# A layer norm with GELU: its last 128 rows as two half tiles, the first of them kept off one DMA engine

## The chip, the cores and the metric

The kernel runs on one core of one Trainium2 chip. The metric is the time of one execution in device microseconds (us), as the median of several executions. A profile of one execution shows a span from the first to the last instruction that is about 1.8 us shorter than the time. All timed runs compared here were at the full granted clock (1.0). Ratios are the mean time of one kernel's fast runs over that of the kernel before in the same rounds, so they are not quite the ratio of the medians that are quoted.

## The reference, cut to what matters

```python
x: (8, 1024, 2048) float32          # 8192 rows of 2048, 8 KB each
normalized = (x - mean(x)) / sqrt(var(x) + eps)     # per row
out = gamma * normalized + beta
return 0.5 * out * (1 + tanh(sqrt(2 / pi) * (out + 0.044715 * out ** 3)))
```

67.1 MB are read and 67.1 MB written.

## The kernel before

The rows are worked on in tiles of 128 rows by 128 partitions. Four tiles (512 rows) are a block; each partition of a block holds four neighbouring rows, 32 KB. Five block buffers (`xts`, "slots") rotate. SyncE loads a block once the store that used its slot has landed; ScalarE issues the stores. VectorE takes the statistics of a tile and scales by gamma, GpSimd raises the variance to the power -1/2, ScalarE normalizes, TensorE adds beta and the scaled tile in PSUM, ScalarE applies the GELU and writes back into the slot.

```python
R = 4                                    # tiles in a block
SLOTS = 5
...
xg = xf.rearrange("(b p r) d -> b p r d", p=P, r=R)
...
@block.sync
def _(sy):
    for b in range(B):                   # B = 16 blocks
        s = slot(b)
        if stored(b):
            sy.wait_ge(s_store[s], stored(b))
        ...
        if b:
            sy.dma_start(out=xts[s], in_=xg[b]).then_inc(s_load[s], 16)
...
@block.scalar                            # the last block's stores go out tile by tile
    if by_row(b):
        ins.then_inc(s_r, 1)
        ac.dma_start(out=og[b, :, q:q + 1], in_=xt[:, q:q + 1])._wait_ge(
            s_r, b + q + 1).then_inc(s_store[slot(b)], 16)
    elif q == R - 1:
        ins.then_inc(s_r, 1)
        ac.dma_start(out=og[b], in_=xt)._wait_ge(s_r, b + 1).then_inc(s_store[slot(b)], 16)
```

## Time and profile before

| | before |
|---|---|
| time, median (before the prediction, 3 runs) | 319.74 us |
| DMA engines | at the top digit in 38 of 40 slices |
| busiest compute engine | VectorE, 83% |
| last store issued | 305.3 us |
| last completion of that store | 316.5 us |

The lines that carry the argument stand in the prediction. One part of the page adds to them. It lists the kinds of transfers: what goes where, issuer, count, size of one, and the median time from issue to landing.

```profile
xt<-in_x_dram SPq DMA_DIRECT2D x15, 4096.0 KB, 24.3
out_dram<-xt ACTq DMA_DIRECT2D x15, 4096.0 KB, 37.0
xt<-in_x_dram SPq DMA_DIRECT2D x4, 1024.0 KB, 8.1
out_dram<-xt ACTq DMA_DIRECT2D x4, 1024.0 KB, 12.7
```

A store of 1 MB needs about 2.5 us of all sixteen engines (eight packets of 309 ns on each), yet lands 12.7 us after its issue: it stands in a queue. I judged that handing over work sooner would not shorten such a tail, and that evening out what the sixteen engines still have to do could.

### The profile page before, as it was taken

The numbers are of one execution on the slowest core, as the hardware profiler recorded it, in microseconds if no ns is written. First come the engines' busy times: TensorE is split into PE (matmuls) and PEld (weight loads), VectorE is DVE, ScalarE is ACT, GpSimd is POOL, SyncE is SP. The second block draws the span as 40 slices with busy tenths as digits, with TensorE's granted clock in tenths as the row PEclk, the third lists the DMA queues.
The fourth block names the chain that finished last, engine by engine and source line by source line (L and its number), as shares of the span: only waits on it lengthen the run. The fifth ranks groups of instructions, "written<-read, shape, count | busy, mean of one in ns | idle before, by whom it ended". The sixth has DMA issues, their size and how long they took to land.

```text
span 317.8 us, 2075 instructions
## 1 busy us (share of the span) xinstructions
PE 244.3 (77%) x520; PEld 57.1 (18%) x520; DVE 265.0 (83%) x514; ACT 253.9 (80%) x132; POOL 79.0 (25%) x73
## 2 busy tenths in 40 slices
PE   2769988888888898888877868598595895868810
PEld 1211222111212122211111111122121111112100
DVE  3499999999999999999969799696996969879500
ACT  2679999999999999999969779696995969968920
POOL 1033323232323231323213222231312213212000
DMA  7999999999999999999999999999999999999994
GB/s 291 438 462 396 459 396 445 412 454 404 458 400 459 422 437 445 412 450 408 458 417 441 437 421 454 404 458 412 450 433 425 450 408 450 408 458 421 437 404 206
DMA packets 5571, 134.27 MB, mean 423 GB/s; under 512 B 656, under 2 KB 704, under 8 KB 704
## 3 DMA queue, kind: packets, MB, share of 16 engines
q1 hardware_dynamic: 2736, 67.11, 49.4%
q10 hardware_dynamic: 2832, 67.13, 49.1%
q14 instruction: 3, 0.02, 0.0%
HBM read 67.13 MB, written 67.11 MB: 422 GB/s over the span
## 4 chain that ended last, share of the span: by engine, by line
DMA 44%; DVE 27%; ACT 19%; PE 3%; issue 2%; ACTq 1%; DVEq 0%; SPq 0%
DMA out_dram<-xt 27%; DVE sts L148 15%; DMA xt<-in_x_dram 15%; ACT yk L201 12%; DVE zg L164 9%; ACT xt L208 7%; PE ps L226 2%; DMA rows<-in_gamma_dram 2%; DVE mvs L157 2%; DVE nms L141 1%; ACTq L216 1%; DVE ves L158 1%; PE ps L243 1%; ACT g_t L197 1%; ACTq L211 0%
## 5 line engine op out<-in xcount | busy, mean ns | idle before, releaser
L148 DVE BATCH_NORM_STATS2 sts<-xt 128x6 f32<-128x512 f32 x256 | 163.5, 681 | 23.7 <-DMA xt<-in_x_dram 21.7
L201 ACT ACTIVATE yk<-xt,nms,rss 128x2048 bf16<-128x2048 f32 x64 | 134.1, 2095 | 41.7 <-DVE nms L141 41.2
L243 PE MATMUL ps<-zg,ident 128*128 128x512 bf16 x256 | 120.8, 627 | 50.9 <-DVE zg L164 50.9
L132 POOL TENSOR_TENSOR rss<-ves,mhalf 128x1 f32<-128x1 f32 x64 | 78.0, 1219 | 216.5 <-DVE ves L158 157.0
L239 PE MATMUL ps<-b_hl,ones_b 33*128 33x512 bf16 x256 | 120.6, 624 | 2.2 <-PEq L234 2.2
L208 ACT ACTIVATE xt<-ps 128x2048 f32<-128x2048 f32 x64 | 118.8, 1857 | 1.5 <-PE ps L243 1.5
L164 DVE TENSOR_TENSOR zg<-yk,g_t 128x2048 bf16<-128x2048 bf16 x64 | 78.0, 1218 | 5.0 <-ACT yk L201 3.0
L243 PEld LDWEIGHTS ps<-zg,ident 128*128 128x128 bf16 x256 | 27.6, 130 | 144.1 <-DVE zg L164 108.7
L239 PEld LDWEIGHTS ps<-b_hl,ones_b 33*128 33x128 bf16 x256 | 27.0, 127 | 92.1 <-issue 88.4
L157 DVE BATCH_NORM_AGGREGATE mvs<-sts 128x2 f32<-128x24 f32 x64 | 16.9, 264 | 2.2
L141 DVE TENSOR_SCALAR nms<-mvs,rss 128x1 f32<-128x1 f32 x64 | 12.6, 196 | 0.0
L226 PE MATMUL ps<-rows,ones 1*128 1x512 f32 x8 | 7.2, 1072 | 6.0 <-DMA rows<-in_gamma_dram 6.0
L158 DVE TENSOR_SCALAR ves<-mvs 128x1 f32<-128x1 f32 x64 | 9.8, 154 | 2.2
L194 ACT ACTIVATE b_hl<-rows 1x2048 bf16<-1x2048 f32 x1 | 1.9, 1909 | 4.9 <-DMA rows<-in_beta_dram 4.9
L226 PEld LDWEIGHTS ps<-rows,ones 1*128 1x128 f32 x8 | 2.5, 323 | 9.2 <-DMA rows<-in_gamma_dram 6.0
L172 DVE TENSOR_TENSOR b_hl<-rows,b_hl 1x2048 bf16<-1x2048 f32 x1 | 2.3, 2281 | 2.1 <-ACT b_hl L195 2.1
L197 ACT ACTIVATE g_t<-ps 128x2048 bf16<-128x2048 f32 x1 | 1.9, 1877 | 2.4 <-PE ps L226 2.4
L190 ACT ACT_TABLE_LOAD x1 | 1.3, 1283 | 0.9 <-SPq L106 0.9
L167 DVE MEMSET b_hl<- 33x1024 uint32 x1 | 0.9, 912 | 1.2 <-SPq L106 1.2
L195 ACT ACTIVATE b_hl<-rows 1x2048 bf16<-1x2048 f32 x1 | 1.9, 1908 | 0.0
L123 POOL MEMSET ones<- 65x128 f32 x1 | 0.2, 202 | 0.5 <-SPq L106 0.5
L127 POOL TENSOR_SCALAR_AFFINE_SELECT ident<-ident 128x128 bf16<-128x128 bf16 x1 | 0.3, 294 | 0.1
(7 smaller groups left out, 0.9 us busy)
## 6 DMA issues: line engine op xcount, KB each, us to landing
xt<-in_x_dram SPq DMA_DIRECT2D x15, 4096.0 KB, 24.3
out_dram<-xt ACTq DMA_DIRECT2D x15, 4096.0 KB, 37.0
xt<-in_x_dram SPq DMA_DIRECT2D x4, 1024.0 KB, 8.1
out_dram<-xt ACTq DMA_DIRECT2D x4, 1024.0 KB, 12.7
rows<-in_beta_dram ACTq DMA_DIRECT2D x2, 8.0 KB, 5.6
rows<-in_gamma_dram ACTq DMA_DIRECT2D x1, 8.0 KB, 5.0
```

The source lines that it names most:

```text
L132: po.tensor_tensor(out=rss[:, c], in0=ves[:, c], in1=mhalf, op=ALU.pow)._wait_ge(s_a, k + 1).then_inc(s_q, 1)
L141: ve.tensor_scalar(out=nms[:, c], in0=mvs[:, q, 0:1], scalar1=rss[:, c], scalar2=-1.0, op0=ALU.mult, op1=ALU.mult)._wait_ge(s_q, count).th ...
L148: ins = ve.bn_stats(out=sts[:, q, j, :], in_=xr[:, j, :])
L157: ve.bn_aggr(out=mvs[:, q], in_=sts[:, q])._wait_ge(s_o, count + 1).then_inc(s_o, 1)
L158: ve.tensor_scalar(out=ves[:, q:q + 1], in0=mvs[:, q, 1:2], scalar1=float(eps), scalar2=1.0, op0=ALU.add, op1=ALU.mult)._wait_ge(s_o, coun ...
L164: ve.tensor_tensor(out=zgs[q % 2], in0=yks[q % 2], in1=g_t, op=ALU.mult)._wait_ge(s_n, count).then_inc(s_z, 1)
L197: ac.activation(out=g_t, in_=pss[0], func=ACT.Identity)._wait_ge(s_tg, 1).then_inc(s_c, 1)
L201: ac.activation(out=yks[t % 2], in_=xts[slot(b)][:, q], func=ACT.Identity, scale=rss[:, q:q + 1], bias=nms[:, q:q + 1])._wait_ge(s_p, t + ...
L208: ins = ac.activation(out=xt[:, q], in_=pss[i % 2], func=ACT.Gelu_apprx_tanh)._wait_ge(s_t, i + 1)
L226: ins = pe.matmul(pss[0][:, cols(j)], lhsT=ones[64:65], rhs=rows[64:65, j * K // nsub:(j + 1) * K // nsub, :d // K], start=True, stop=True)
L239: ins = pe.matmul(ps[:, cols(j)], lhsT=ones_b, rhs=b_hl[:, cols(j)], start=True, stop=False)
L243: ins = pe.matmul(ps[:, cols(j)], lhsT=ident, rhs=zgs[k % 2][:, cols(j)], start=False, stop=True)
```

## The change

The intent is to even out the engines at the end. The last 128 rows are worked on as two half tiles of 64 rows. Of the first half 60 rows go through one transfer and 4 rows through another: fifteen engines with four rows each and four engines with one row each. So one engine loads and stores four rows fewer than it did. The second half is spread over all sixteen engines (16 updates with data). It needs a 65th step of every compute engine, and a load that waits for one more slot.

```diff
+H = 64
+E = 4
...
+    def halves(v, a, h):
+        return [(v[n1:n1 + H - E], a[32:32 + H - E]), (v[n1 + H - E:n1 + H], a[0:4 * E:4]),
+                (v[n1 + H:n1 + 2 * H], h[32:32 + H])]
...
-                    if b:
+                    if 0 < b < B - 1:
                         sy.dma_start(out=xts[s], in_=xg[b]).then_inc(s_load[s], 16)
+                        if s == slot(B - 1):
+                            sy.sem_inc(s_tail, 32)
+                sy.dma_start(out=x_end[:, :R - 1], in_=last(xf)).then_inc(s_load[slot(B - 1)], 16)
+                for v, a in x_half[:2]:
+                    sy.dma_start(out=a, in_=v).then_inc(s_tail, 16)
+                sy.wait_ge(s_store[slot(B)], stored(B))
+                sy.dma_start(out=x_half[2][1], in_=x_half[2][0]).then_inc(s_load_h, 16)
...                                  # one more step on GpSimd, VectorE, ScalarE and TensorE
+                        for k, (v, a, se) in enumerate(outs[i]):
+                            dma = ac.dma_start(out=v, in_=a)
+                            if k == 0:
+                                dma._wait_ge(s_r, n_r)
+                            dma.then_inc(se, 16)
```

More of the change, by code (lines that the diff above doesn't have):

```diff
@@ L38, with last @@
     og = of.rearrange("(b p r) d -> b p r d", p=P, r=R)
+    n0 = n - P * R
+    n1 = n0 + P * (R - 1)
+    def last(v):
+        return v[n0:n1].rearrange("(p r) d -> p r d", p=P)
+    def halves(v, a, h):
+        return [(v[n1:n1 + H - E], a[32:32 + H - E]), (v[n1 + H - E:n1 + H], a[0:4 * E:4]),
+                (v[n1 + H:n1 + 2 * H], h[32:32 + H])]
     bf16 = mybir.dt.bfloat16
@@ L70 @@
     s_first = [sem(f"first{q}") for q in range(R)]
+    s_tail = sem("tail")
+    s_load_h = sem("load_h")
+    s_half = sem("half")
     s_load = [sem(f"load{s}") for s in range(SLOTS)]
@@ L98, in cols, with parts @@
         return slice(j * FMAX, (j + 1) * FMAX)
-    def by_row(b):
-        return b == B - 1
+    def parts(b):
+        return R + 1 if b == B - 1 else 1
     def stored(b):
-        return sum(16 * (R if by_row(c) else 1) for c in range(b) if slot(c) == slot(b))
+        return sum(16 * parts(c) for c in range(b) if slot(c) == slot(b))
+    tiles = [xts[slot(b)][:, q] for b in range(B) for q in range(R)] + [xts[slot(B)][:, 0]]
+    n_t = len(tiles)
+    x_end = xts[slot(B - 1)]
+    x_half, o_half = halves(xf, x_end[:, R - 1], tiles[-1]), halves(of, x_end[:, R - 1], tiles[-1])
+    outs = {R * b + R - 1: [(og[b], xts[slot(b)], s_store[slot(b)])] for b in range(B - 1)}
+    for q in range(R - 1):
+        outs[n_t - 1 - R + q] = [(last(of)[:, q:q + 1], x_end[:, q:q + 1], s_store[slot(B - 1)])]
+    outs[n_t - 2] = [(v, a, s_store[slot(B - 1)]) for v, a in o_half[:2]]
+    outs[n_t - 1] = [(v, a, s_half) for v, a in o_half[2:]]
     with tc.tile_critical(no_gpsimd_drain=True):
@@ L128, in _, with power @@
                                  pattern=[[-1, P]], channel_multiplier=1)._wait_ge(s_setp, 1).then_inc(s_setp, 1)
+                def power(t, count):
+                    c = slice(t % R, t % R + 1)
+                    po.tensor_tensor(out=rss[:, c], in0=ves[:, c], in1=mhalf,
+                                     op=ALU.pow)._wait_ge(s_a, count).then_inc(s_q, 1)
                 with po.Fori(0, B):
                     for k in range(R):
-                        c = slice(k, k + 1)
-                        po.tensor_tensor(out=rss[:, c], in0=ves[:, c], in1=mhalf,
-                                         op=ALU.pow)._wait_ge(s_a, k + 1).then_inc(s_q, 1)
+                        power(k, k + 1)
                     po.sem_inc(s_a, -R)
+                power(n_t - 1, 1)
             @block.vector
@@ L142, in mean, with step @@
                                      op0=ALU.mult, op1=ALU.mult)._wait_ge(s_q, count).then_inc(s_p, 1)
-                def step(s, q, wait, count, before, count_q, count_n):
-                    xr = xts[s][:, q].rearrange("p (s f) -> p s f", f=FMAX)
+                def step(x, q, wait, count, before, count_q, count_n):
+                    xr = x.rearrange("p (s f) -> p s f", f=FMAX)
                     for j in range(nsub):
@@ L151, in step @@
                                 ins._wait_ge(*wait)
-                                if wait[0] is s_load[s]:
-                                    ins.then_inc(s_load[s], -16)
+                                if wait[0] not in s_first:
+                                    ins.then_inc(wait[0], -wait[1])
                             if before is not None:
@@ L168, in _ @@
                 for q in range(R):
-                    step(slot(0), q, (s_first[q], 16), 2 * q, q - 1 if q else None, q, q)
+                    step(tiles[q], q, (s_first[q], 16), 2 * q, q - 1 if q else None, q, q)
                     if q == 0:
@@ L180, in _ @@
                         s, q = divmod(k, R)
-                        step(s, q, (s_load[s], 16) if q == 0 else None, 2 * k, (q - 1) % R, k + 1, k + 1)
+                        wait = (s_load[s], 16) if q == 0 else (s_tail, 32) if (s, q) == (slot(B - 1), R - 1) else None
+                        step(xts[s][:, q], q, wait, 2 * k, (q - 1) % R, k + 1, k + 1)
                     ve.sem_inc(s_o, -2 * SLOTS * R)
@@ L184, in _ @@
                     ve.sem_inc(s_n, -SLOTS * R)
-                mean(R - 1, 1)
-                scale(R - 1, 1)
+                step(tiles[-1], 0, (s_load_h, 16), 0, R - 1, 1, 1)
+                mean(0, 2)
+                scale(0, 2)
             @block.scalar
@@ L197, in _ @@
                 ac.activation(out=g_t, in_=pss[0], func=ACT.Identity)._wait_ge(s_tg, 1).then_inc(s_c, 1)
-                for t in range(T + 1):
-                    if t < T:
-                        b, q = divmod(t, R)
-                        ac.activation(out=yks[t % 2], in_=xts[slot(b)][:, q], func=ACT.Identity, scale=rss[:, q:q + 1],
-                                      bias=nms[:, q:q + 1])._wait_ge(s_p, t + 1).then_inc(s_n, 1)
+                n_r = 0
+                for t in range(n_t + 1):
+                    if t < n_t:
+                        c = slice(t % R, t % R + 1)
+                        ac.activation(out=yks[t % 2], in_=tiles[t], func=ACT.Identity, scale=rss[:, c],
+                                      bias=nms[:, c])._wait_ge(s_p, t + 1).then_inc(s_n, 1)
                     i = t - 1
@@ L205, in _ @@
                         continue
-                    b, q = divmod(i, R)
-                    xt = xts[slot(b)]
-                    ins = ac.activation(out=xt[:, q], in_=pss[i % 2], func=ACT.Gelu_apprx_tanh)._wait_ge(s_t, i + 1)
-                    if by_row(b):
+                    ins = ac.activation(out=tiles[i], in_=pss[i % 2], func=ACT.Gelu_apprx_tanh)._wait_ge(s_t, i + 1)
+                    if i in outs:
                         ins.then_inc(s_r, 1)
-                        ac.dma_start(out=og[b, :, q:q + 1], in_=xt[:, q:q + 1])._wait_ge(
-                            s_r, b + q + 1).then_inc(s_store[slot(b)], 16)
-                        ac.sem_inc(s_g, 1)
-                    elif q == R - 1:
-                        ins.then_inc(s_r, 1)
-                        ac.dma_start(out=og[b], in_=xt)._wait_ge(s_r, b + 1).then_inc(s_store[slot(b)], 16)
+                        n_r += 1
+                        for k, (v, a, se) in enumerate(outs[i]):
[3 more added lines that the diff above has]
+                            dma.then_inc(se, 16)
                         ac.sem_inc(s_g, 1)
@@ L234, in _, with summed @@
                 pe.sem_inc(s_g, 2)
+                def summed(t, count):
+                    ps, zg = pss[t % 2], zgs[t % 2]
+                    for j in range(nsub):
+                        ins = pe.matmul(ps[:, cols(j)], lhsT=ones_b, rhs=b_hl[:, cols(j)], start=True, stop=False)
+                        if j == 0:
+                            ins._wait_ge(s_g, count)
+                    for j in range(nsub):
+                        ins = pe.matmul(ps[:, cols(j)], lhsT=ident, rhs=zg[:, cols(j)], start=False, stop=True)
+                        if j == 0:
+                            ins._wait_ge(s_z, count)
+                    ins.then_inc(s_t, 1)
                 with pe.Fori(0, B):
                     for k in range(R):
-                        ps = pss[k % 2]
-                        for j in range(nsub):
-                            ins = pe.matmul(ps[:, cols(j)], lhsT=ones_b, rhs=b_hl[:, cols(j)], start=True, stop=False)
-                            if j == 0:
-                                ins._wait_ge(s_g, k + 1)
-                        for j in range(nsub):
-                            ins = pe.matmul(ps[:, cols(j)], lhsT=ident, rhs=zgs[k % 2][:, cols(j)],
-                                            start=False, stop=True)
-                            if j == 0:
-                                ins._wait_ge(s_z, k + 1)
-                        ins.then_inc(s_t, 1)
+                        summed(k, k + 1)
                     pe.sem_inc(s_g, -R)
                     pe.sem_inc(s_z, -R)
+                summed(n_t - 1, 1)
+        nc.gpsimd.wait_ge(s_half, 16)
         for b in range(B, B + SLOTS):
```

## The prediction

> **What bounds the kernel now.** I read the page first, for which engine is full, and then the last 60 us in finer stretches, because the change touches only the last block of rows.
>
> ```profile
> PE 244.3 (77%) x520; PEld 57.1 (18%) x520; DVE 265.0 (83%) x514; ACT 253.9 (80%) x132; POOL 79.0 (25%) x73
> ...
> DMA  7999999999999999999999999999999999999994
> ...
> HBM read 67.13 MB, written 67.11 MB: 422 GB/s over the span
> ```
>
> The first row gives the busy time of each engine. None reaches 84%. The DMA row is at its top digit in every slice but the first and the last. So the transfers are the bound from end to end: 134.2 MB through 16 DMA engines. The packet records of the trace give the pace: a packet of 8 KB (one row) takes 309 ns, and one of 32 KB (four rows of one partition) takes 1213 ns. Each engine moves 512 rows in and 512 out; 1024 times 0.303 us is 310 us, which is nearly the span of 317.8. VectorE, ScalarE and TensorE matter only if they hand over a store too late. The end shows they don't:
>
> ```profile
> 300.20 1.23 DVE L164 TENSOR_TENSOR zg<-yk,g_t 128x2048 bf16<-128x2048 bf16 x1 [3.00 <-ACT yk L201]
> ...
> 303.41 1.88 ACT L208 ACTIVATE xt<-ps 128x2048 f32<-128x2048 f32 x1 [1.48 <-PE ps L243]
> 305.32 0.34 ACTq L211 DMA_DIRECT2D out_dram<-xt  x1
> ```
>
> (Timeline: start, length, what.) The last arithmetic ends at 305.3 and the last store is issued there, yet the span runs for 12.5 us more. That time is the queue of stores draining. How it drains is the view that matters here (stretches; the last two columns are the mean busy share of the 16 DMA engines and GB/s):
>
> ```profile
> core 0: us, PE busy (x) PEld busy (x) DVE busy (x) ACT busy (x) POOL busy (x), PEclk, DMA share, GB/s
> ...
> 312.00:313.00 1.00, 0.00 (x0) 0.00 (x0) 0.00 (x0) 0.00 (x0) 0.00 (x0) 1.00 1.04 442
> 313.00:314.00 1.00, 0.00 (x0) 0.00 (x0) 0.00 (x0) 0.00 (x0) 0.00 (x0) 1.00 0.43 180
> 314.00:315.00 1.00, 0.00 (x0) 0.00 (x0) 0.00 (x0) 0.00 (x0) 0.00 (x0) 1.00 0.12 49
> 315.00:316.00 1.00, 0.00 (x0) 0.00 (x0) 0.00 (x0) 0.00 (x0) 0.00 (x0) 1.00 0.12 49
> 316.00:317.00 1.00, 0.00 (x0) 0.00 (x0) 0.00 (x0) 0.00 (x0) 0.00 (x0) 1.00 0.00 0
> ```
>
> The reader is to see 0.12 from 314 to 316: 0.12 times 16 is 1.9, so **two** engines still work while fourteen are done. The 16 completions of the last store say the same: fourteen fall between 313.71 and 314.22 us, the last two at 316.39 and 316.50. The final packets of the two late engines end at 316.06, within 10 ns of each other; those of the others end between 313.3 and 313.9. The delay is about 2.2 us, seven to eight packets of 8 KB. From the last completion to the end of the span it is a fixed 1.3 us. So the most that any rebalancing of the last rows can bring is about 2.2 us of 319.7, **0.7%**.
>
> [...] The kernel before has only 16-way transfers (each completion count has 16 steps that come with the data), so its trace cannot confirm the other cases.
> [...]
>
> **The change part by part.**
> - *Rows taken from engine 15.* It loads and stores 4 rows fewer: 8 packets of 309 ns, **-2.47 us** on that engine. That is just the delay seen (2.2 us), so I take this to be the intent.
> - *Rows given to engines 0 to 3.* One row in and one out each: +0.62 us. Their end moves from at most 313.9 to about 314.5.
> - *More transfers.* The last block was one load and four stores; it is now four loads and six stores (three rows per partition in one load, then 60, 4 and 64 rows; stores of three full tiles, 60, 4 and 64). Successive transfers show gaps of some 75 ns on an engine in the packet records at some ends. As an estimate, three extra on a typical engine cost 0.2 us, and five on engines 0 to 3 cost 0.4 us. Smaller packets: eight of 32 KB take 9.70 us; eight of 24 KB (0.91 us each, interpolated from 309 and 1213 ns) plus eight of 8 KB take 9.76 us. That is +0.06 us.
> - *One more tile of arithmetic.* A half tile costs an engine as much as a full one[...]: four statistics of 0.69 us, 0.26, 0.15, 0.20 and 1.23 on VectorE, about 4.2 us; 2.1 and 1.86 on ScalarE. Stores of the last tiles were issued at 293.26, 297.61, 301.97 us, so 4.35 us apart. In the worst case the last store slips from 305.3 to 309.7.
> - *Loads come in another order.* The last block's load was issued at 255.76 and landed at 279.96; VectorE idled 2.57 us for it. Behind the previous load (259.1) the three-row part needs eight turns of 0.91 + 1.21 us, so it lands at about 276 to 277.6. VectorE is free at 277.5, so tile 60 starts some 2.5 us earlier. The 60 rows then take four turns of 0.31 + 1.21 us, landing near 282, the last 64 rows near 288 to 290; tiles 63 and 64 are due at about 290 and 295. The last load also waits for a store that landed at 275.1; that is in time. So the last store should be issued near 307 and 309.7 at the latest.
> - *Is the drain starved?* Before the last 64 rows, the engines have work until about 312.4 (313.6 less four packets). A store issued at 307 to 309.7 is in time. The extra tile lies beside the draining stores and costs nothing.
>
> Sum by engine, last packet: typical engines 313.6 + 0.3 = 313.9; engines 0 to 3 about 314.6 to 314.9; engine 15, if late, 316.06 - 2.47 + 0.3 = 313.9; the **other late engine 316.06 + 0.3 = 316.3, if nothing else changes for it**.
>
> **The rivals.**
> (a) *The second straggler sets the end.* It has the same end as the first and keeps its work, so the time stays within 0.3 us of before: about 319.9. For it: the completions of the last seven stores each show two late engines, about 2 us behind. Against it: the author moved rows off one engine only[...]. The second one's delay may also belong to this execution: in the stores of blocks landing up to 117 us only one engine is late, and the second appears after.
> (b) *Only engine 15 matters, or the two delays hang together*, so that relief for one relieves the other. For it: the two reach the same end within 10 ns. Then engines 0 to 3 set the end, near 314.6 to 314.9, that is 1.2 to 1.5 us earlier: about 318.4.
> (c) *Arithmetic becomes the bound.* If the late loads slip by over 3 us, the last store comes too late and the end moves out by as much: 320 to 322. Against it is the slack of 2.7 us or more worked out above.
> (d) *The odd transfers are slow.* 60 partitions on fifteen engines is a shape that nothing in this trace shows. If it ran on far fewer engines, a single engine would have to move many rows at 0.31 us each, and the time would rise by 2 us or more.[...]
>
> **Range and chances.** I give (a) 0.45, (b) 0.42, and (c) and (d) together 0.13. That puts the middle at **319.2 us**, with 318.0 to 320.3 as the range for 8 times in 10. A gain over 2% would need 6.4 us, three times the whole tail, and a loss over 2% a serious failure of (c) or (d). So faster 0.01, same 0.98, slower 0.01.
>
> **What would show it.** In the last stretches: one engine left (a share near 0.06 for about 1.5 us) means (a); a share that falls to 0.25 or less for only half a microsecond (engines 0 to 3) and an end near 315 means (b). In the timeline, tile 60's statistics should start near 277.5 and the last store be issued between 307 and 309.7; a DMA share below 0.9 between 295 and 312 means (c). Landing times of the 60-row load and store far over those of the 64-row ones mean (d). The prediction is wrong if the late engines turn out not to be slow by themselves but late through something that the new order moves, or if the last arithmetic starves the drain.

The sum came to 319.2 us, with the last packets at 313.9 us on a typical engine, 314.6 to 314.9 on engines 0 to 3, 313.9 on engine 15 and 316.3 on the other late one. That the four engines are 0 to 3, and that the spared one is engine 15, was my assumption. The traces show only how many engines a transfer uses. Engine numbers in this document are labels from the first experiment: engine k - 1 is the one that a small load of k rows is the first to reach. The "turns" of a load's and a store's packet are my estimate, from the two queues' shares of the engines' time before (49.4% and 49.1%, page of the kernel before).

## The result, and the profile after

The time is 319.81 us (319.68 to 320.18, 6 runs) against 319.71 us before (6 runs). The ratio is 1.0002, with a 95% interval of 0.9989 to 1.0015. The change moves the time by nothing that can be seen.

First the timeline of the end of the changed kernel (start, length, engine, line, what):

```profile
302.70 1.23 DVE L206 TENSOR_TENSOR zg<-yk,g_t 128x2048 bf16<-128x2048 bf16 x1 [2.99 <-ACT yk L246]
...
306.06 1.88 ACT L251 ACTIVATE xt<-ps 128x2048 f32<-128x2048 f32 x1 [1.63 <-PE ps L286]
307.97 0.59 ACTq L256 DMA_DIRECT2D out_dram<-xt  x1
```

The 65th step costs nothing: the last store goes out 2.65 us later than before, and the engines still have work. Then the drain, in the same stretches and columns as in the prediction (the last two are the DMA share and GB/s):

```profile
312.00:313.00 1.00, 0.00 (x0) 0.00 (x0) 0.00 (x0) 0.00 (x0) 0.00 (x0) 1.00 0.95 401
313.00:314.00 1.00, 0.00 (x0) 0.00 (x0) 0.00 (x0) 0.00 (x0) 0.00 (x0) 1.00 0.61 254
314.00:315.00 1.00, 0.00 (x0) 0.00 (x0) 0.00 (x0) 0.00 (x0) 0.00 (x0) 1.00 0.22 90
315.00:316.00 1.00, 0.00 (x0) 0.00 (x0) 0.00 (x0) 0.00 (x0) 0.00 (x0) 1.00 0.12 49
316.00:317.00 1.00, 0.00 (x0) 0.00 (x0) 0.00 (x0) 0.00 (x0) 0.00 (x0) 1.00 0.00 0
```

The share of 0.12 from 315 to 316 is still there: two engines work while the others are done, just as before. What changed is the stretch from 314 to 315, where 0.22 (3.5 engines) stands in place of 0.12: the engines that took over the four rows. The sixteen completions of the last store tell the rest. A completion is one of the sixteen updates of the transfer's semaphore; in the kernel before, the last two came 0.3 and 0.4 us after the last packets ended (316.06). They come from the trace, sorted; they carry no engine numbers. (In the kernel before, the tile stores share one semaphore, so two of the values near 314 are late completions of the store ahead; which two cannot be seen.)

```
before   313.71 ... 314.22 (fourteen)                                      316.39  316.50
changed  311.68   313.82 ... 314.10 (ten)   314.48  315.04  315.09         316.45  316.66
```

One engine is now done 2.1 us ahead of all others. By the change that is the engine which the 60 rows spare, engine 15 in the prediction: it alone has less to do. Eight packets of 309 ns are 2.47 us, and 311.68 + 2.47 is 314.15, just after the pack of ten. So the spared engine was not among the late two before, and the two that were late still are. My first reading was then: **the change relieves an engine that was not late.** Three things had to be tested: which engines are late, whether the relief does anything, and what makes an engine late.

### The profile page after: what moved, and what is told of

Read it like the earlier page. It is cut to its first block, busy times and chain, and to the rows that moved or that the text cites. A ratio compares the mean times of both kernels' runs of the same rounds, so it can differ in the third digit from the quotient of the medians.

```text
span 317.9 us, 2115 instructions
## 1 busy us (share of the span) xinstructions
PE 248.0 (78%) x528; PEld 58.1 (18%) x528; DVE 269.2 (85%) x522; ACT 257.7 (81%) x134; POOL 79.5 (25%) x74
## 3 DMA queue, kind: packets, MB, share of 16 engines
q1 hardware_dynamic: 2899, 67.11, 49.4%
## 4 chain that ended last, share of the span: by engine, by line
DMA 43%; DVE 27%; ACT 21%; PE 2%; issue 2%; ACTq 2%; DVEq 0%; SPq 0%
DMA out_dram<-xt 26%; DVE sts L190 15%; DMA xt<-in_x_dram 15%; ACT yk L246 13%; ACT xt L251 8%; DVE zg L206 8%; PE ps L269 2%; DMA rows<-in_gamma_dram 2%; DVE mvs L199 2%; ACTq L256 2%; DVE nms L183 1%; DVE ves L200 1%; ACT g_t L241 1%; ACTq L260 0%; DVEq L220 0%
## 5 line engine op out<-in xcount | busy, mean ns | idle before, releaser
L190 DVE BATCH_NORM_STATS2 sts<-xt 128x6 f32<-128x512 f32 x260 | 165.9, 679 | 22.1 <-DMA xt<-in_x_dram 19.8
L246 ACT ACTIVATE yk<-xt,nms,rss 128x2048 bf16<-128x2048 f32 x65 | 136.1, 2093 | 40.4 <-DVE nms L183 39.9
L286 PE MATMUL ps<-zg,ident 128*128 128x512 bf16 x260 | 122.7, 627 | 49.6 <-DVE zg L206 49.6
L282 PE MATMUL ps<-b_hl,ones_b 33*128 33x512 bf16 x260 | 122.5, 624 | 2.2 <-PEq L277 2.2
L251 ACT ACTIVATE xt<-ps 128x2048 f32<-128x2048 f32 x65 | 120.6, 1856 | 1.6 <-PE ps L286 1.6
L206 DVE TENSOR_TENSOR zg<-yk,g_t 128x2048 bf16<-128x2048 bf16 x65 | 79.2, 1219 | 5.0 <-ACT yk L246 3.0
```

Source lines behind the costliest of these rows:

```text
L190: ins = ve.bn_stats(out=sts[:, q, j, :], in_=xr[:, j, :])
L206: ve.tensor_tensor(out=zgs[q % 2], in0=yks[q % 2], in1=g_t, op=ALU.mult)._wait_ge(s_n, count).then_inc(s_z, 1)
L246: ac.activation(out=yks[t % 2], in_=tiles[t], func=ACT.Identity, scale=rss[:, c], bias=nms[:, c])._wait_ge(s_p, t + 1).then_inc(s_n, 1)
L251: ins = ac.activation(out=tiles[i], in_=pss[i % 2], func=ACT.Gelu_apprx_tanh)._wait_ge(s_t, i + 1)
L282: ins = pe.matmul(ps[:, cols(j)], lhsT=ones_b, rhs=b_hl[:, cols(j)], start=True, stop=False)
L286: ins = pe.matmul(ps[:, cols(j)], lhsT=ident, rhs=zg[:, cols(j)], start=False, stop=True)
```

## The experiments

**1. Which engines are late.** Sixteen small loads were put at the end of ScalarE's queue, behind the stores. The k-th has k rows and a semaphore of its own.

```diff
+    probe = sb("probe", [16, 16 * 128], f32)
...
+                for k in range(1, 17):
+                    ac.dma_start(out=probe[0:k, (k - 1) * 128:k * 128], in_=xf[0:k, 0:128]).then_inc(s_probe[k], 16)
```

> The kernel before, with sixteen small loads at the very end of the ScalarE queue; the k-th one reads k rows of 512 bytes into k partitions and counts on a semaphore of its own[...], behind all stores of that queue. The first k whose completions hold a late one (near 316 us, when the others are near 314) names the first late engine; the k at which a second late one joins names the second. Theory 1 (the late engines are those that also carried instruction fetches): two late engines, and engine 15 is not among them, so the late count is the same for k = 15 and k = 16. [...] The time rises by 1 to 3 us from the extra issues.

(What could be tested of the second theory, that engine 15 is late, is that the late count would rise at k = 16.)

The run was correct and took 322.8 us. The completions that came with data were, in us:

```
k=1   314.47
k=2   314.51  314.67
k=3   313.95  314.69  314.85
k=4   314.12  314.86  315.02  315.61
k=5   314.31  315.03  315.20  315.80  317.07
k=6   314.04  314.48  315.20  315.41  315.99  317.25
```

Each list repeats the one above about 0.17 us later, as the small loads queue on an engine, and has one new value. At k = 4 the new value is 315.61 in place of about 314: engine 3 is late. At k = 5 it is 317.07: engine 4 is late, and later. Up to k = 15 nobody else is; engine 7's value, new at k = 8, is 314.07.

The list of k = 16 tests engine 15 itself: its six values above 315.99 each continue one of k = 15, about 0.2 us later, so the new one is at 315.99 or earlier. An engine as late as the two of the kernel before (316.39) would have come after that. The load was issued too late to say more.

The kernel before had just two late completions, so they are those of **engines 3 and 4**. The lists up to k = 15 also have exactly k values that came with data, so a transfer of k rows did run on k engines. That these are the lowest numbers the trace does not show; 3, 4 and 15 are labels. That the engine which the 60 rows spare is the one that only the load of 16 rows reaches is not shown either. That it is neither engine 3 nor engine 4, the next probe tells.

The same probe was added to the changed kernel.

> The changed kernel with the sixteen small loads at the end that told engine numbers in the kernel before (engine 3 late by 1.4 us, engine 4 by 2.2 us or more, engine 15 with the rest). If the reading is right: engines 3 and 4 are late again, engine 3 by 0.6 us more than engine 4's change, since the four extra rows fell on engines 0 to 3, and engine 15 alone is early, some 2 us ahead of the rest. If engine 15 were the late one in the kernel before, it would now be with the rest. Time 1 to 3 us above the changed kernel from the extra issues.

It took 324.16 us. At k = 4 the new value was 316.94, where the three others lay between 314.92 and 315.73; at k = 5 engine 4 joined (317.13 and 317.19 are the two late ones), at k = 6 the new one came at 314.82. The last half tile's store had one completion at 311.76 and its two last at 316.75 and 316.96. So engines 3 and 4 are late in the changed kernel too, and the spared engine, early by itself, is another. Engine 3 is, if my assumption holds, among the four that received a row more, and has now nearly caught up with engine 4 in lateness: 316.94 against 315.61 is 1.3 us, twice the 0.62 us of a row in and out, and near the 1.0 us of the prediction's row and extra transfers together. My expectation of one early engine, alone, holds (311.76); from k = 6 on the small loads were issued too late to test whether it is engine 15.

**2. Does the relief of engine 15 do anything?** The 60 + 4 rows were made 64 rows over all engines.

```diff
-        return [(v[n1:n1 + H - E], a[32:32 + H - E]), (v[n1 + H - E:n1 + H], a[0:4 * E:4]),
-                (v[n1 + H:n1 + 2 * H], h[32:32 + H])]
+        return [(v[n1:n1 + H], a[32:32 + H]), (v[n1 + H:n1 + 2 * H], h[32:32 + H])]
```

> The changed kernel without its relief of engine 15: the last 128 rows as 64 + 64 rows, both over all sixteen engines. If engine 15 is not a late one: the time is within 0.3 us of the changed kernel and of the kernel before (319.5 to 320.1 us), no completion of the last store comes early (in the changed kernel one came at 311.68 us, 2.1 us ahead of the rest), and two come late by about 2.2 us. If engine 15 is a late one: the last completion is later than in the changed kernel by up to 2.5 us, and so is the time. The four rows on engines 0 to 3 fall away too, so if one late engine is among them, the time falls by up to 0.6 us.

Measured: 319.84 us (5 runs, 319.63 to 320.18), ratio 1.0006 (0.9993 to 1.002). Its drain:

```profile
313.00:314.00 1.00, 0.00 (x0) 0.00 (x0) 0.00 (x0) 0.00 (x0) 0.00 (x0) 1.00 0.63 262
314.00:315.00 1.00, 0.00 (x0) 0.00 (x0) 0.00 (x0) 0.00 (x0) 0.00 (x0) 1.00 0.12 49
315.00:316.00 1.00, 0.00 (x0) 0.00 (x0) 0.00 (x0) 0.00 (x0) 0.00 (x0) 1.00 0.06 25
```

Fourteen completions come between 313.86 and 314.39 us, none early, and two late, at 315.39 and 316.57. Without the extra row on four engines the less late of the two ends 1.1 us sooner (0.06, one engine, in the last stretch), but the other one keeps its 316.57 and with it the time. So neither the relief nor the four rows matter to the end: it belongs to one engine, by the probe engine 4, to which the change gives and takes no row as far as its end shows (316.66 with it, 316.57 here).

**3. What makes an engine late?** The trace has three packets of 8 KB on the queue of instructions during the run, at 34.3, 99.5 and 109.9 us, of 0.31 to 0.33 us each. I call them fetches. My theory was that they set an engine back, that is, that they add to its lag. An engine's lag is the time by which its completion comes after the middle one of the sixteen. That a packet holds 128 instructions was an estimate; the padded SyncE program below bears it out, with four packets for 512 added instructions, as does the padded ScalarE program with two for 260. If one goes out for each 128 instructions of a program, VectorE (226 instructions, counted in the program and not in the trace) accounts for two and ScalarE (190) for one. The rival was that engines 3 and 4 are slow whatever they carry. Two kernels got more fetches. In the first, ScalarE increments an unread semaphore four times per tile:

```diff
+                    for _ in range(4):
+                        ac.sem_inc(s_pad, 1)
```

> The kernel before with four semaphore increments, of a semaphore that nobody reads, per tile on ScalarE: 190 instructions become 450. If ScalarE's instruction fetches go as packets of 8 KB (128 instructions)[...], the instruction queue shows 5 to 6 packets during the run in place of 3. Theory 1 (each fetch sets one engine back by some 1.2 us for good): the same engine takes all of ScalarE's fetches, and its lag at the end grows from 2.2 to 4 us or more, and the time by 1.5 to 3.5 us, to 321.3 to 323. Theory 2 (the lag is a property of the engine): the lag stays at 2.2 us and the time within 0.4 us of before, as ScalarE has the slack for 0.2 us more per tile.

Measured: 320.33 us, ratio 1.0018 (1.0002 to 1.0033); five instruction packets during the run, at 34.3, 53.1, 99.5, 133.6 and 228.6; last completion 317.20 us, 3.15 us behind the middle one of the sixteen (before: 316.50, 2.57 behind). That is between the two theories: 0.6 us more lag for two more fetches, and less time than I expected. Nor is it one engine that takes it all, as I had expected: the completions at 315.61 and 316.19 are late by 1.6 and 2.1 us, so three engines are late here and not two.

In the second, SyncE makes 128 increments after each of four loads:

```diff
                         sy.dma_start(out=xts[s], in_=xg[b]).then_inc(s_load[s], 16)
+                    if 6 <= b < 10:
+                        for _ in range(128):
+                            sy.sem_inc(s_pad, 1)
```

> The kernel before with 128 such increments on SyncE after each of the loads 6 to 9, where SyncE only waits: 41 instructions become 553, which by the same count makes four more fetches (7 instruction packets in all during the run), between 80 and 160 us. Theory 1: a third late engine appears, or one of the two is set back further, by some 3 to 5 us in all; the last completion moves out by 1 to 3 us and the time to 320.7 to 323. Theory 2: as before, 319.7 within 0.4 us, two late engines by 2.2 us.

Measured: **323.75 us**, ratio 1.0128 (1.0112 to 1.0143), the largest effect. The new instruction packets came at 88.9, 107.6, 127.5 and 148.1 us. The first fence is the count of transfers by queue (packets, MB, share), the second SyncE's waits for landed stores (us, times, longest) in the kernel before and then in this one, the third the drain:

```profile
q14 instruction: 7, 0.06, 0.0%
```

```profile
SPq L119 <- DMA out_dram<-xt: 247.1, 11, 55.6
SPq L120 <- DMA out_dram<-xt: 217.8, 11, 57.2
```

```profile
314.00:315.00 1.00, 0.00 (x0) 0.00 (x0) 0.00 (x0) 0.00 (x0) 0.00 (x0) 1.00 0.45 188
315.00:316.00 1.00, 0.00 (x0) 0.00 (x0) 0.00 (x0) 0.00 (x0) 0.00 (x0) 1.00 0.06 25
316.00:317.00 1.00, 0.00 (x0) 0.00 (x0) 0.00 (x0) 0.00 (x0) 0.00 (x0) 1.00 0.06 25
317.00:318.00 1.00, 0.00 (x0) 0.00 (x0) 0.00 (x0) 0.00 (x0) 0.00 (x0) 1.00 0.06 25
318.00:319.00 1.00, 0.00 (x0) 0.00 (x0) 0.00 (x0) 0.00 (x0) 0.00 (x0) 1.00 0.08 33
319.00:320.00 1.00, 0.00 (x0) 0.00 (x0) 0.00 (x0) 0.00 (x0) 0.00 (x0) 1.00 0.06 25
```

Here 0.06, one engine, works alone for five microseconds. Its last completion is at 320.58, and the middle of the sixteen at 314.9. The middle is some 1.0 us later than in the kernel before, presumably because each load waits for a whole landed store, the late part included (not tested). SyncE still waited before eleven loads, as in the kernel before, so its increments held no load back.

Which engine is it? The probe was added to this kernel.

> The padded SyncE program with the sixteen small loads at the end. Theory 1: SyncE's four extra fetches fall on one DMA engine, so one engine number is late by 5 to 6 us; engines 3 and 4 are late too. If it is engine 3 or 4 again, the lag is that engine's own and not the fetches'; if it is one that was not late in the kernel before, the fetches made it late. I expect another engine than 3 and 4, with 0.75. Time 324 to 327.

It took 326.96 us. At k = 5 the new value was 321.21, while k = 4 had brought 315.61: it is **engine 4** again, now 7.0 us behind, with engine 3 at its old lag. My guess of another engine (0.75) was wrong. SyncE's fetches fall on an engine that was late already. That leaves the rival alive, that engine 4 is slow by itself, but the rival cannot explain why it falls 3.1 us further behind (5.7 us behind the middle instead of 2.6) when only SyncE's program grew. A control had to show that it is the length of the program and not SyncE's activity. So the increments were put in a loop, which was to need no fetch (the 24-turn version below has the three packets of the kernel before):

```diff
+                    if 6 <= b < 9:
+                        with sy.Fori(0, 80):
+                            sy.sem_inc(s_pad, 1)
```

> The control for the padded SyncE program: SyncE makes 80 increments after each of the loads 6 to 8, but in a loop of one increment, so its program has 56 instructions and needs no fetch. Theory 1 (the fetches cost the time): three instruction packets during the run, the time of the kernel before, 319.7 within 0.4 us. Rival (the increments themselves, or SyncE being busy beside the transfers, cost the time): 321 us or more.

Measured: 324.07 us, ratio 1.0126. At face value that kills the theory; the profile says it is no control. A turn of the loop takes about 0.3 us (SyncE waited 83.7 us less than in the kernel before, over 240 turns; in the next control 22.6 us less, over 72), so SyncE was away for some 25 us and issued loads late. SyncE's waits show it, and so do the digits of the DMA row near the end:

```profile
SPq L120 <- DMA out_dram<-xt: 163.4, 7, 55.9
```

```profile
DMA  7999999999999999999999999999999999994797
```

Only seven loads had to wait for a store; the others went out after the slot had long been free. The missing work appears as a hole of the transfers (4 and 7 tenths) some 16 to 32 us before the end. At the end no engine is late at all (all sixteen completions within 0.2 us), presumably because the hole let all catch up (not tested). The time went to starvation, another cause. The control was repeated with 24 turns.

> The control again, since the first one (80 turns) held SyncE for 25 us per load, so that loads went out late and the DMA engines stood idle near the end. Now 24 turns, some 7 us per load, about what the padded program took (its SyncE waited 29 us less in all, over four loads), after the loads 6 to 8; 56 instructions, so no fetch by SyncE. Theory 1 (the fetches set engine 4 back): SyncE still waits for a landed store ahead of each load, as in the kernel before; three instruction packets; two late engines, by 1.4 and 2.2 us; the time 319.7 within 0.4 us. Rival (a busy SyncE costs the time, not its fetches): 321 us or more, with loads still on time.

Measured: 320.19 us, ratio 1.0016 (0.9999 to 1.0033). The same lines for it:

```profile
q14 instruction: 3, 0.02, 0.0%
```

```profile
SPq L120 <- DMA out_dram<-xt: 224.5, 11, 55.5
```

```profile
314.00:315.00 1.00, 0.00 (x0) 0.00 (x0) 0.00 (x0) 0.00 (x0) 0.00 (x0) 1.00 0.16 66
315.00:316.00 1.00, 0.00 (x0) 0.00 (x0) 0.00 (x0) 0.00 (x0) 0.00 (x0) 1.00 0.08 33
316.00:317.00 1.00, 0.00 (x0) 0.00 (x0) 0.00 (x0) 0.00 (x0) 0.00 (x0) 1.00 0.00 0
```

Eleven waits of nearly the same sum as in the padded program (224.5 against 217.8 us), but three instruction packets instead of seven. The last completion lies 2.6 us behind the middle, not 5.7. (A third engine is late by 1.1 us at the end; a lag of that size is in its stores from 60 us on, before the first loop.) So of the 4 us of the padded program SyncE's activity explains about 0.5 us (up to 1 us by the interval). The rest, about 0.9 us for each of the four fetches, came with them, though such a packet takes only 0.31 us itself.

The control is not a full match: it makes 72 increments and not 512. The traces close that gap, as they show when a lag grows. Here is the lag of the latest completion in four loads of each run (landing time of the middle completion, then the lag, both in us):

```
first probe     32: 0.45    45: 1.85    84: 1.83   103: 2.81   fetches at 34.3 and 99.9
padded SyncE   105: 1.60   124: 2.78   143: 4.02   163: 4.94   fetches at 107.6, 109.4, 127.5, 148.1
control        103: 2.77   123: 2.76   142: 2.71   162: 2.71   one fetch, at 109.0
```

In the padded program the lag grows by 0.9 to 1.2 us from each load to the next, with one of SyncE's fetches between them. In the first probe, without a single added increment, it grows by 1.4 and 1.0 us across VectorE's two fetches and not between them. The control stays flat. ScalarE's fetch at 109.0 makes no step in this list, and on which engine it falls is not seen. An engine that is slow by itself at a steady rate would grow late between the fetches too.

**4. Attempts at a faster version.** Three moved the programs in instruction memory, so that, by my guess at which instruction a fetch goes out, some of ScalarE's and VectorE's fetches would come before the transfers fill the engines.

```diff
+                ac.addr_align(256, offset=66, max_nops=0)
                 ac.preload_act_table(ACT.Gelu_apprx_tanh)
...
+                ve.addr_align(256, offset=84, max_nops=0)
                 ve.memset(b_hl, 0.0).then_inc(s_m, 1)
```

> The kernel before with the same instructions, only placed elsewhere in instruction memory[...]. [...] during the run one is left for VectorE (near 60 us) and one for ScalarE (near 225 us instead of 109 us): two instruction packets in place of three. Theory 1 (a fetch sets its DMA engine back for good, and what carries ScalarE's then drifts): engine 3 is late by some 0.7 us in place of 1.4, engine 4 by some 1.3 us in place of 2.2; the last completion comes about 0.9 us sooner and the time is 318.5 to 319.2, faster than both kernels. Theory 2 (engines 3 and 4 are late by themselves, whatever they carry): lags and time as before, 319.7 within 0.3 us.[...]

> Only ScalarE's program moved (slot 66). Theory 1: VectorE's two fetches stay near 34 and 100 us, so one engine is late by 1.4 us as in the kernel before; ScalarE's moves from 109 to about 225 us, and the engine that was last (2.2 us late) is late by 1.3 us or less; the end moves up by 0.7 to 0.9 us, time 318.8 to 319.1. Theory 2: 319.7, two late engines as before.

> Only VectorE's program moved (slot 84). Theory 1: the engine that is last is ScalarE's, so the end stays and the time is 319.7 within 0.2 us, but the other late engine's lag halves to about 0.7 us. Theory 2: no lag changes.

All three missed, though the last one's time was as forecast. With VectorE's program moved, its fetches came at 30.8 and 97.4 us, hardly sooner than before (34.3 and 99.5); ScalarE's stayed at 108.9; the lags were 1.2 and 2.5 us and the time 319.76 us (ratio 1.0001). So my picture of when a fetch goes out was wrong, but the two fetches that moved were VectorE's, which confirms whose they are. With ScalarE's program moved, the start stalled: two extra packets came at 1.8 and 7.9 us, gamma's load took until 9.8 us to be issued and the first block store went out at 46.5 us in place of 36.4. The transfers ran short early on (this is the row of GB/s in 40 slices):

```profile
GB/s 292 443 437 443 402 452 390 313 354 447 443 378 390 440 424 435 435 427 439 435 423 439 439 423 439 439 419 443 439 419 443 435 419 447 435 419 443 439 394 244
```

313 and 354 in the eighth and ninth slice, 378 and 390 in the twelfth and thirteenth, are lost transfer time. The times were 322.89 us (ratio 1.0082) and, with both moved, 321.84 us (1.0093). They say nothing on the theory, as the stall hides it.

The last attempt aimed at engines 3 and 4 themselves. In the probe, each small load issued from ScalarE reached all engines of the smaller ones: those of 5 rows and more reached engines 3 and 4 too. So I saw no way to spare these two with a transfer from ScalarE and still use the others. GpSimd's way of issuing was tried instead.

```diff
+                for k, q in enumerate((R - 2, R - 1)):
+                    po.dma_start(out=dummy[:, k * 128:(k + 1) * 128], in_=xf[0:5, 0:128]).then_inc(s_dum[k], 16)
+                    po.dma_start(out=og[B - 1, 80:124, q:q + 1], in_=xts[slot(B - 1)][80:124, q:q + 1])._wait_ge(
+                        s_r, B + q).then_inc(s_sw[k], 16)
...
-                        ac.dma_start(out=og[b, :, q:q + 1], in_=xt[:, q:q + 1])._wait_ge(
+                        for k, (lo, hi) in enumerate([(0, P)] if q < R - 2 else [(0, 80), (124, 127), (127, 128)]):
```

> The kernel before with relief for the engines that are late. Each of the last two tile stores is cut into 80 rows on all sixteen engines, 3 rows on engines 0 to 2, 1 row on engine 0 and 44 rows issued from GpSimd. A small GpSimd load over five partitions goes ahead of each[...]. Then engines 3 and 4 store 6 rows fewer (1.85 us), engines 5 to 15 two more (0.6 us). If it works: engine 4 ends 0.3 us after, engine 3 ahead of the others, which set the end at about 314.6 in place of 316.1; time 318.3 to 318.9, faster than both kernels by some 0.3 to 0.4%.[...]

(Cut are two guesses at the engines on which GpSimd's rows fall, with the time of 319.7 to 320.7 us that went with the second. The engines of the rows that remain are assumed, not shown.)

It was slower: 322.03 us, ratio 1.0092 (1.0064 to 1.012), with single runs from 320.9 to 324.1. In the profiled one the last completion of the stores came at 317.48 us, and it was one of ScalarE's own pieces; GpSimd's stores had all landed by 315.2. On which engines GpSimd's 44 rows fell, the trace does not tell. No version beats the kernel before.

## Why the prediction was right or wrong

The time, 319.81 us, lies in the range, and the class "same" had 0.98. The middle, 319.2, was a mean of two cases; the measured time is that of rival (a), which said 319.9. That hit is partly luck: (a) has one of two late engines relieved, and in fact neither was. The end is the same in both cases, as one late engine is enough to set it.

- **DMA bound, drain to the end, two late engines, at most 0.7% to gain:** right. Two late engines also show in the profiles of the changed kernel, of the even halves and of the probes on both kernels. That the two ended within 10 ns of each other, which I held in favour of (b), belongs to that execution: in the first probe's run, the same program with the small loads behind it, the lags were 1.4 and 2.9 us.
- **"Rows taken from engine 15": -2.47 us on that engine:** right in size, as far as the completion at 311.68 can tell, which is 2.1 to 2.4 us ahead of the pack.
- **"That is just the delay seen (2.2 us), so I take this to be the intent":** this is the step that failed. An equal size was taken as a sign that engine 15 was one of the two late engines, which no trace showed. The probe names engines 3 and 4. So my sum "engine 15, if late, 316.06 - 2.47" applied to no engine, and case (b), at 0.42, could not happen in any form.
- **The other late engine at 316.3, "if nothing else changes for it":** right; the last packets ended at 316.12 and 316.20. For the reason above there were two such engines and not one. My sign for (a), a share of 0.06, was therefore off; the share stayed at 0.12.
- **Engines 0 to 3 at 314.6 to 314.9:** near for three of them. Their completions are at 314.48 to 315.09, and a completion comes some 0.3 to 0.5 us after the last packet, for which the sum stands (316.45 and 316.66 after 316.12 and 316.20). That the fourth may be a late engine, engine 3, which the change then burdened further (316.94 at k = 4 in the probe), I did not see.
- **The 65th step is hidden:** right. VectorE began tile 60 at 278.24 (I said 277.5), the last store was issued at 307.97 (307 to 309.7). The turns between the two queues were counted rightly for most engines: the 60 rows came in from 282.2 (near 282), the last half tile from 288.3 (288 to 290). But a load has landed only with its last completion, and I forgot the late engines there. With the 4 rows that share their semaphore, the 60 rows were complete at 286.95, and the last half tile at 294.24, over 4 us after my figure. VectorE took that tile up at 295.16, so the slack was 0.9 us and not several. Rivals (c) and (d) fell, (c) by less than I thought.

What stays open: the four added fetches set engine 4 back; the control and the steps of its lag show that. In the unpadded kernel only one of the two lags is accounted for. In the trace of the first probe the lag of one engine steps up across VectorE's fetches at 34.3 and 99.9 us. The other engine's lag, in its loads, grows slowly from 0.8 us at 123 to 2.1 us at 278, across no fetch, and I have no account of that growth. It is this one that sets the end, as far as the lists can tell: it goes on smoothly in the stores (2.2 us at 273, 2.5 at 294, 2.9 at 314), while the stepped one is at 1.4 us there. So what makes the unpadded kernel's last engine late is not shown. Nor do I know why a packet of 0.31 us costs 0.9.

## What to carry to other kernels

When a transfer-bound kernel ends on a few late DMA engines, first find their numbers, for instance with small transfers of 1, 2, 3 and more rows on semaphores of their own, and only then shift rows; relief for an engine that is not among the last was worth nothing here (319.81 against 319.71 us), and one late engine that kept its work kept the time (316.57 us at its end, 319.84 us in all, with the even halves). A match in size between a delay and a relief is no proof that they concern the same engine. A longer program can also cost transfer time (here 1.3% for 512 instructions, with four more packets on the instruction queue and one DMA engine 5.7 us behind the middle instead of 2.6); and a control is worth reading in its own profile before it is believed.
